# An adding transfer in place of a subtraction: remainders of every second half block of up weights

## The chip, the cores and the metric

The kernel runs on one core of a Trainium2 chip. The metric is the time of one execution in device microseconds (us); the figure for a kernel is the median of several runs. The core has five engines with instruction queues of their own, each working through its queue in order: TensorE (PE; its weight loads are listed as PEld), VectorE (DVE), ScalarE (ACT), GpSimd (POOL) and SyncE (SP). Transfers are issued from the queues of SP, ACT or POOL and carried by 16 DMA engines, which all queues share.

## The reference

Two layers of an encoder over 256 tokens of width 2048. Each layer computes a joint input projection, two groups of attention heads, an output projection, and then a gated feed-forward with a short convolution over the tokens:

```python
h2 = rms_norm(x, ln2_g[l])
u = depthwise_conv(h2 @ w_up[l], conv_w[l], conv_b[l])
gate, up = u[..., :D_FF], u[..., D_FF:]
x = x + (jax.nn.silu(gate) * up) @ w_down[l]
```

`w_up` has 2048 rows and 2 x 5632 columns in each layer. All data are float32. The change concerns only how the blocks of `w_up` are prepared for TensorE.

## The kernel before

All products run on TensorE in the type float32r, which keeps fewer bits than float32. To hold the precision, each operand is taken apart into a rounded part and a remainder: hi = round(w), lo = w - hi. A product is then the sum of hi·hi, hi·lo and lo·hi; each half block of weights is therefore needed as two tiles, `whi` and `wlo`.

The weights come in blocks of 128 x 2048 elements (1 MB), the *quanta*. The list `quanta` (lines 700 to 730) fixes their order for the whole kernel: for each layer 36 blocks of the input projection, 16 of the output projection, then in five chunks the blocks of up (two for each of 44 column blocks f), and between them those of down in three kinds (`plain`, `seven`, and the ordinary ones). Each quantum is worked off in two *steps* of half a block, 1024 columns, a `seven` in three. A step of up weights is eight pairs of matmuls (`two`, lines 411 to 414): one of 512 columns with a piece of `whi` and one of 256 columns with a piece of `wlo`.

What precedes a step's matmuls:

- `load` (line 736) loads a quantum into one of three `raw` buffers by a transfer of SP's queue. The next load is issued when the last step of the quantum has been split (`left`, lines 768 to 771), three quanta ahead.
- `split_w` (line 753) takes a half block apart: it fetches a `whi` and a `wlo` buffer, of which there are five each (`SPLIT_AHEAD + 1`), and calls `split` (line 109). There ACT rounds the half block into `whi` (line 112) and DVE subtracts this from the raw block into `wlo` (line 113).
- The main loop (lines 854 to 860) calls `split_w` four steps ahead of the matmuls. The buffers that step s + 4 gets are those that step s - 1 has read, so the rounding waits for TensorE to finish step s - 1.

After the last step of a column block f, `glu` (line 540) takes the result out of the accumulator (ACT, L546; DVE, L547 and L548), copies the edges of the convolution on POOL (L550, L551), convolves (ACT, L556; DVE, L558), applies the gate (L560, L562) and splits the result for the down products. Apart from these copies POOL computes some powers (L107) and sums of squares (L124) in the attention stage; it issues no transfer.

The order on each engine is worked out by the planner of the tile framework, from the program's order, its estimate of durations and the priorities set with `tc.high_priority`. `split_w` sets such a priority around the splitting (line 760). The framework also derives the waits from what each instruction reads and writes.

Of the kernel before, what the change touches and what calls it, by code (L numbers as in the profile page):

```python
# [12 lines left out]
F32R = mybir.dt.float32r  # L13
I32 = mybir.dt.int32
AF = mybir.ActivationFunctionType
ALU = mybir.AluOpType
# [43 lines left out]
def encoder_kernel(  # L60
# [5 lines left out]
    nc = tc.nc  # L66
# [42 lines left out]
    def split(hi, lo, src, scale=None):  # L109

        if scale is None:
            high = nc.scalar.activation(hi, src, AF.Copy)  # L112
            nc.vector.tensor_sub(lo, src, hi.bitcast(F32))  # L113
        else:
            high = nc.scalar.activation(hi, src, AF.Copy, scale=scale)  # L115
            nc.vector.scalar_tensor_tensor(lo, src, scale, hi.bitcast(F32),
                                           op0=ALU.mult, op1=ALU.subtract)
        return high
# [286 lines left out]
    quanta = []  # L405
# [122 lines left out]
    def q_up(l, f, u):  # L528
        def body(q, half, hi, lo):
            if u == 0 and half == 0:  # L530
                cur["up"] = psum.tile([P, 2, 2, T], F32, name="mm", bufs=2)
            ps = cur["up"]
            hv, lv = (w.rearrange("p (k j n) -> p k j n", k=4, j=2) for w in (hi, lo))
            for j in range(2):
                for kk in range(4):
                    k = 8 * u + 4 * half + kk
                    two(ps[:, j], hv[:, kk, j], lv[:, kk, j], xs[k], k == 0, k == KD - 1)
            if u == 1 and half == 1:
                glu(l, f, ps)
        return body  # L540
# [159 lines left out]
    for l in range(L):  # L700
# [8 lines left out]
        for c, nf in enumerate(CHUNKS):  # L709
            up = lambda f: [(a["w_up"][l, f, u], q_up(l, f, u), "up") for u in range(2)]  # L710
# [23 lines left out]
    raw, hl, left, loads, highs = {}, {}, {}, {}, {}  # L734

    def load(q, parts=1):
        if q < len(quanta):
            raw[q] = wp.tile([P, 2048], F32, name="raw", bufs=3)
            left[q] = 3 if quanta[q][2] == "seven" else 2
            m = 2048 // parts  # L740
            for j in range(parts):
                loads[q] = nc.sync.dma_start(out=raw[q][:, j * m:(j + 1) * m], in_=quanta[q][0][:, j * m:(j + 1) * m])

    def split_seven(w, part, hi, lo):

        hv, lv = (t.rearrange("p (k n) -> p k n", k=2) for t in (hi, lo))
        if part == 1:
            nc.vector.tensor_sub(w[:, 1:3], w[:, 1:3], w[:, 2:4])
            nc.vector.tensor_add(w[:, 3], w[:, 3], w[:, 1])
            nc.vector.tensor_sub(w[:, 0], w[:, 3], w[:, 0])  # L750
        return split(hv, lv, (w[:, 1::2], w[:, 1:3], w[:, 0::3])[part])

    def split_w(s, parts=1):
        if s < len(steps):
            q, half = steps[s]
            kind = quanta[q][2]
            o = UP_AT if kind == "up" else 0
            hl[s] = tuple(wp.tile([P, 1024 + 64], F32R, name=t, bufs=SPLIT_AHEAD + 1)[:, o:o + 1024]
                          for t in ("whi", "wlo"))
            with tc.high_priority(offset=AHEAD_PRIO if s >= KD // 2 else 0):  # L760
                if kind == "seven":
                    highs[s] = split_seven(raw[q].rearrange("p (k n) -> p k n", k=4), half, *hl[s])
                else:
                    m = 1024 // parts
                    for j in range(parts):
                        highs[s] = split(*(t[:, j * m:(j + 1) * m] for t in hl[s]),
                                         raw[q][:, half * 1024 + j * m:half * 1024 + (j + 1) * m])
            left[q] -= 1
            if left[q] == 0:
                del raw[q]  # L770
                load(q + LOAD_AHEAD)
# [65 lines left out]
    for i in range(SPLIT_AHEAD):  # L837
        first_x(i)
        split_w(i, 2 if i == 0 else 1)
# [14 lines left out]
    for s, (q, half) in enumerate(steps):  # L854
        if s + SPLIT_AHEAD < KD // 2:
            first_x(s + SPLIT_AHEAD)
        split_w(s + SPLIT_AHEAD)
        quanta[q][1](q, half, *hl.pop(s))
        for f, args in side.pop((q, half), []):
            f(*args)  # L860
# [101 lines left out]
```

## Time and profile before

| | |
|---|---|
| runs | 2090.13, 2090.67, 2090.73 us; median 2090.67 |
| span of the profiled execution | 2088.2 us, first to last instruction; the profile has no other time of that execution |
| DMA engines | 408.41 MB moved, mean 196 GB/s over the span |
| loads of up weights | 176 of 1024 KB, all on SP's queue |
| steps of up weights | 352, 8 x 352 = 2816 matmuls of each of the two sizes |

The profile is one execution. Busy time is the union of an engine's instructions; for TensorE the ends of pipelined matmuls are modelled, so the waits and the pace say more there than the share. "L113" is line 113 of the kernel. In the groups, `wlo<-raw,whi` means that `wlo` is written from `raw` and `whi`, `x795` is the count (a few records are missing), then busy us and mean ns, then the idle time of the engine before these instructions with what ended it.

### The profile page before, as it was taken

The page shows a single profiled execution, that of the slowest core. Times are in us where ns is not written, and L with a number is a line of the kernel's source. Part 1 is how long each engine was busy: PE and PEld are TensorE (multiplying, and loading weights), DVE is VectorE, ACT ScalarE, POOL GpSimd, SP SyncE. Part 2 cuts the span into 40 slices and gives each one's busy share as a digit, 9 for nine tenths or more (in the row PEclk, how much of TensorE's full clock was granted, in tenths as well). Part 3 has the DMA queues.
Part 4 walks back from the last instruction along what each step waited for, and adds up shares of the span by engine and source line. Part 5 has one row for each costly group of instructions (what it writes and reads, how often), then busy time and mean ns, then how long its engine had stood idle before and what let it go on. Part 6 is the DMA issues. An engine that isn't in the chain of part 4 may idle for free.

```text
span 2088.2 us, 29195 instructions
## 1 busy us (share of the span) xinstructions
PE 2082.8 (100%) x10816; PEld 1788.6 (86%) x10816; DVE 1719.4 (82%) x2604; ACT 1222.1 (59%) x1817; POOL 175.4 (8%) x237
## 2 busy tenths in 40 slices
PE   9999999999999999999999999999999999999999
PEld 8888888888888888888888888888888888888887
DVE  7786657898898988989757766578989989899896
ACT  7566556555555556556555665565656565555553
POOL 0011100100101001011000111001001010010100
PEclk9999999999999999999999999999999999999999
DMA  9544555556565564656655445555565655656554
GB/s 353 196 144 168 176 179 173 194 200 207 179 242 184 209 211 165 240 194 210 208 182 182 162 166 171 169 180 195 208 202 175 235 195 204 204 187 232 184 200 161
DMA packets 62143, 408.41 MB, mean 196 GB/s; under 512 B 7344, under 2 KB 9904, under 8 KB 13744
## 3 DMA queue, kind: packets, MB, share of 16 engines
q1 hardware_dynamic: 61280, 405.46, 56.4%
q8 instruction: 85, 1.39, 0.3%
q10 hardware_dynamic: 720, 1.08, 0.2%
q14 instruction: 58, 0.48, 0.1%
HBM read 404.42 MB, written 2.10 MB: 195 GB/s over the span
## 4 chain that ended last, share of the span: by engine, by line
PE 100%; ACT 0%; DVE 0%; issue 0%
PE mm L98 90%; PE S L98 4%; PE pv L98 3%; PE tr L98 2%; PE tr L373 1%; PE tr L307 1%; PE S L149 1%; ACT v_a L263 0%; ACT mid L115 0%; DVE x L689 0%; DVE ones L90 0%; DVE halfpi L94 0%; DVE power L92 0%
## 5 line engine op out<-in xcount | busy, mean ns | idle before, releaser
L112 ACT ACTIVATE whi<-raw 128x1024 fp32r<-128x1024 f32 (+1 forms) x797 | 830.8, 1057 | 684.3 <-PE mm L98 403.0
L113 DVE TENSOR_TENSOR wlo<-raw,whi 128x1024 fp32r<-128x1024 f32 (+1 forms) x797 | 964.8, 1221 | 271.9 <-ACT whi L112 234.6
L98 PE MATMUL mm<-xs,whi 128*128 128x512 f32 x2816 | 977.0, 390 | 0.0
L98 PE MATMUL mm<-xs,wlo 128*128 128x256 f32 x2816 | 794.1, 282 | 0.0
L98 PEld LDWEIGHTS mm<-xs,whi 128*128 128x128 f32 x2816 | 528.3, 188 | 110.5
L98 PEld LDWEIGHTS mm<-xs,wlo 128*128 128x128 f32 x2816 | 532.2, 189 | 1.1
L98 PE MATMUL mm<-whi,mid 128*128 128x512 f32 x1412 | 369.4, 391 | 0.4 <-ACT v_a L263 0.4
L98 PEld LDWEIGHTS mm<-whi,mid 128*128 128x128 f32 x1412 | 262.6, 188 | 54.5 <-ACT v_a L263 0.9
L98 PE MATMUL mm<-whi,xs 128*128 128x512 f32 x1152 | 294.7, 393 | 0.1
L98 PEld LDWEIGHTS mm<-whi,xs 128*128 128x128 f32 x1152 | 212.7, 188 | 42.6 <-ACT whi L112 0.8
L98 PE MATMUL mm<-wlo,mid 128*128 128x512 f32 x706 | 201.8, 391 | 0.0
L98 PE MATMUL mm<-wlo,xs 128*128 128x512 f32 x576 | 158.8, 392 | 0.0
L98 PEld LDWEIGHTS mm<-wlo,mid 128*128 128x128 f32 x706 | 132.2, 188 | 27.2
L558 DVE SCALAR_TENSOR_TENSOR pT<-halo,conv,pT 128x256 f32<-128x256 f32 x352 | 148.3, 480 | 0.9
L550 POOL COPY halo<-halo 128x6 f32<-128x6 f32 x88 | 40.6, 461 | 1233.6 <-DVE halo L548 1233.6
L98 PEld LDWEIGHTS mm<-wlo,xs 128*128 128x128 f32 x576 | 107.0, 188 | 21.4
L556 ACT ACTIVATE pT<-halo,conv 128x256 f32<-128x256 f32 x176 | 95.1, 588 | 5.8 <-DVE halo L548 5.7
L551 POOL COPY halo<-halo 128x6 f32<-128x6 f32 x88 | 76.0, 864 | 0.2 <-POOL halo L550 0.2
L548 DVE TENSOR_TENSOR halo<-prob,acc_b 128x512 f32<-128x512 f32 x88 | 60.7, 690 | 1.9
L547 DVE TENSOR_TENSOR prob<-prob,mm 128x512 f32<-128x512 f32 x88 | 60.0, 681 | 0.0
L546 ACT ACTIVATE prob<-mm 128x512 f32<-128x512 f32 x88 | 51.4, 584 | 7.1 <-PE mm L98 7.1
L560 ACT ACTIVATE prob<-pT 128x256 f32<-128x256 f32 x88 | 35.6, 404 | 30.3 <-DVE pT L558 30.3
(180 smaller groups left out, 1479.8 us busy)
## 6 DMA issues: line engine op xcount, KB each, us to landing
raw<-in_w_up SPq DMA_DIRECT2D x176, 1024.0 KB, 4.9
raw<-in_w_in SPq DMA_DIRECT2D x71, 1024.0 KB, 4.9
raw<-in_w_down SPq DMA_DIRECT2D x48, 1024.0 KB, 4.9
raw<-in_w_seven SPq DMA_DIRECT2D x40, 1024.0 KB, 4.9
raw<-in_w_out SPq DMA_DIRECT2D x32, 1024.0 KB, 4.8
raw<-in_w_plain SPq DMA_DIRECT2D x10, 1024.0 KB, 4.8
bias<-in_bias SPq DMA_DIRECT2D x16, 160.0 KB, 3.1
x<-in_x SPq DMA_DIRECT2D x4, 512.0 KB, 10.0
```

Of the source, the lines that this page charges most:

```text
L98: nc.tensor.matmul(ps, lhsT, rhs, start=start, stop=stop, skip_group_check=True)
L112: high = nc.scalar.activation(hi, src, AF.Copy)
L113: nc.vector.tensor_sub(lo, src, hi.bitcast(F32))
L149: nc.tensor.transpose(ps[:, j, tt * P:(tt + 1) * P], x[:, tt, (k + j) * P:(k + j + 1) * P], ident)
L546: nc.scalar.activation(t, ps[:, :, 0], AF.Copy)
L547: nc.vector.tensor_add(t, t, ps[:, :, 1])
L548: nc.vector.tensor_mul(ux[:, :, r:r + T], t, st["r2"][:, None, :].to_broadcast([P, 2, T]))
L550: nc.gpsimd.tensor_copy(ux[:, :, 1:r], ux[:, :, T:T + r - 1])
L551: nc.gpsimd.tensor_copy(ux[:, :, T + r:T + 2 * r - 1], ux[:, :, r + 1:2 * r])
L556: nc.scalar.activation(y[:, j, :], ux[:, j, r:r + T], AF.Identity, scale=w1, bias=b)
L558: nc.vector.scalar_tensor_tensor(y[:, j, :], ux[:, j, o:o + T], w, y[:, j, :], op0=ALU.mult, op1=ALU.add)
L560: nc.scalar.activation(t[:, 0, :], y[:, 0, :], AF.Silu)
```

## The change

In `split_w`, the second half (`half == 1`) of every quantum of kind "up" takes a path of its own; all other half blocks keep `split`.

```diff
             with tc.high_priority(offset=AHEAD_PRIO if s >= KD // 2 else 0):
                 if kind == "seven":
                     highs[s] = split_seven(raw[q].rearrange("p (k n) -> p k n", k=4), half, *hl[s])
+                elif kind == "up" and half == 1:
+                    hi, lo = hl[s]
+                    src = raw[q][:, 1024:2048]
+                    highs[s] = nc.scalar.activation(hi, src, AF.Copy)
+                    nc.scalar.activation(lo, src, AF.Copy, scale=-1.0)
+                    nc.gpsimd.dma_start(out=lo, in_=quanta[q][0][:, 1024:2048].bitcast(F32R), accum_op=ALU.add)
                 else:
                     m = 1024 // parts
```

ACT rounds the half block into `whi` as before, and then once more with the sign turned into `wlo`, which then holds -hi. In place of DVE's subtraction, a transfer issued on POOL's queue reads the same half block from device memory (128 rows of 4 KB, 512 KB) and adds it to `wlo`: w + (-hi). There are 2 layers x 44 column blocks x 2 quanta = 176 such half blocks. The transfer waits for the second rounding, and the matmuls that read `wlo` wait for the transfer. The raw buffer is now read by the two roundings alone.

## The prediction

> **What bounds the kernel now.** I read the page's totals and the chain that ended last, then who waited for whom on TensorE, then the stage of the up weights instruction by instruction. The totals and the chain:
>
> ```profile
> span 2088.2 us, 29195 instructions
> PE 2082.8 (100%) x10816; PEld 1788.6 (86%) x10816; DVE 1719.4 (82%) x2604; ACT 1222.1 (59%) x1817; POOL 175.4 (8%) x237
> PEclk9999999999999999999999999999999999999999
> PE 100%; ACT 0%; DVE 0%; issue 0%
> ```
>
> TensorE (PE) is the whole chain. It is not busy for 2088.2 - 2082.8 = 5.4 us, at the granted clock's top tenth throughout. Since the ends of matmuls are modelled, a full PE could hide slow matmuls, so I look for waits of PE and for its pace. The waits on PE and PEld:
>
> ```profile
> PE pv L98 <- DVE halfpi L94: 1.1, 1, 1.1
> PE mm L98 <- ACT v_a L263: 0.4, 2, 0.2
> PEld mm L98 <- ACT whi L112: 0.8, 2, 0.5
> ```
>
> Columns: total us, times, longest. Out of 352 up steps no matmul waited for wlo, and the whole list stays under 4 us. The pace stands in ScalarE's (ACT's) timeline of one up stage, since each rounding there starts when TensorE gives a buffer back:
>
> ```profile
> 503.85 1.06 ACT L112 ACTIVATE whi<-raw 128x1024 fp32r<-128x1024 f32 x1 [1.40 <-issue]
> 504.81 0.58 ACT L546 ACTIVATE prob<-mm 128x512 f32<-128x512 f32 x1
> 506.63 1.06 ACT L112 ACTIVATE whi<-raw 128x1024 fp32r<-128x1024 f32 x1 [1.24 <-PE mm L98]
> 507.60 1.08 ACT L556 ACTIVATE pT<-halo,conv 128x256 f32<-128x256 f32 x2
> 509.39 1.06 ACT L112 ACTIVATE whi<-raw 128x1024 fp32r<-128x1024 f32 x1 [0.72 <-ACT pT L556]
> ...
> 512.18 1.06 ACT L112 ACTIVATE whi<-raw 128x1024 fp32r<-128x1024 f32 x1 [1.42 <-PE mm L98]
> ...
> 514.94 1.06 ACT L112 ACTIVATE whi<-raw 128x1024 fp32r<-128x1024 f32 x1 [0.78 <-ACT mid L112]
> ```
>
> Roundings start at 503.85 and 514.94, four steps apart: 11.09 us, so a step is 2.77 us and a 1 MB up block (two steps) 5.55 us. The 176 up blocks take 176 x 5.55 = 976 us of the span. ACT and VectorE (DVE) prepare each half block four steps ahead (SPLIT_AHEAD, five buffers), so **11.09 us from the freed buffer to the matmul that reads it** is the budget of a half block. Before, it uses 1.06 us for the rounding and 1.22 us for the subtraction.
>
> **What goes away.** The group table, one row a shape:
>
> ```profile
> L113 DVE TENSOR_TENSOR wlo<-raw,whi 128x1024 fp32r<-128x1024 f32 x795 | 963.5, 1223 | 271.8 <-ACT whi L112 234.6 <-PE mm L98 29.3 <-ACT mid L115 3.8
> L112 ACT ACTIVATE whi<-raw 128x1024 fp32r<-128x1024 f32 x795 | 829.7, 1058 | 684.3 <-PE mm L98 403.0 <-DVE raw L748 88.8 <-issue 87.0
> ```
>
> 2 layers x 44 column blocks x 2 blocks x one second half = 176 subtractions of 1.223 us leave DVE: -215 us, 1719 to about 1504 (72%). DVE is not on the chain and TensorE did not wait for it, so this is worth nothing directly; what would be late next is TensorE itself. The most that any shortening can bring is that 5.4 us gap. I count **0**.
>
> **What ACT gets.** 176 more 128x1024 roundings, priced by the row above: 176 x 1.058 = +186 us, 1222 to 1408 (67%). In the stage of up weights ACT has room:
>
> ```profile
> 726.00:820.00 94.00, 94.00 (x537) 83.01 (x536) 82.31 (x126) 54.25 (x79) 8.38 (x14) 1.00 0.60 205
> ```
>
> (Columns: stretch, its us, then busy us of PE, PEld, DVE, ACT, POOL; granted clock; share of the 16 DMA engines; GB/s.) ACT is 54.25 of 94 us, 58%; one more rounding per 5.55 us adds 19 points, 77%. The budget covers it: **0**, but ACT works in order, so the second rounding can stand behind the two L556 of 1.08 us together that follow the one at 506.63. If that cover is gone the half block is ready 1.08 us later; that is a term below. The raw buffer is now given back by this rounding, 2.12 us after the start, where the subtraction gave it back at 1.06 + 1.22 = 2.28: SP's next load is released 0.2 us earlier, worth nothing by itself. But **the same event now releases both the load of 1 MB and the adding transfer**, so they run against each other.
>
> **What POOL and its queue get.** 176 DMA issues, each behind a wait for ACT. The trace of before has no transfer of POOL and none that adds. Queued behind the waiting issue on POOL are the halo copies; DVE's L558 waits for those, and behind L558 on DVE stand the first halves' subtractions. These have 11.09 us and need 2.28, so a POOL held up for a few us costs nothing. The nearest rows for the issue and its surroundings:
>
> ```profile
> L742 SPq DMA_DIRECT2D raw<-in_w_up x176: 327/328/328, 303.8 to 2011.9; - x176
> 507.62 0.19 POOL L550 COPY halo<-halo 128x6 f32<-128x6 f32 x1 [9.03 <-DVE halo L548]
> 507.74 1.26 POOL L551 COPY halo<-halo 128x6 f32<-128x6 f32 x1
> 507.73 1.23 DVE L113 TENSOR_TENSOR wlo<-raw,whi 128x1024 fp32r<-128x1024 f32 x1 [0.24 <-ACT whi L112]
> ```
>
> An issue takes SP 0.33 us. The second copy equals the first in size and takes 1.26 us, exactly while a subtraction of 1.23 us runs on DVE: POOL can be held for one DVE instruction. So an issue is 0.33 to 0.33 + 1.26 = 1.59 us; I take both ends along. The Trainium skill, "SBUF — State Buffer", "Who interferes with whom", says more narrowly that two-input subtractions hold POOL's reads only, and that the writing of descriptors for POOL's transfers is held by DVE's two-port modes (it calls this inferred). By that rule the issue would lie at the low end and the sum below at its low end, by the copy's row at its high end; no row of this trace shows an issue on POOL.
>
> **The transfer.** Its nearest rows, and the transfer engines in this stage and when full:
>
> ```profile
> raw<-in_w_up SPq DMA_DIRECT2D x176, 1024.0 KB, 4.9
> bias<-in_bias SPq DMA_DIRECT2D x16, 160.0 KB, 3.1
> x<-in_x SPq DMA_DIRECT2D x4, 512.0 KB, 10.0
> 499.00:510.00 11.00, 11.00 (x66) 9.74 (x65) 9.29 (x15) 6.35 (x10) 1.38 (x2) 1.00 0.60 194
> 30.00:41.00 11.00, 11.00 (x50) 9.11 (x49) 10.62 (x27) 9.13 (x17) 0.73 (x1) 1.00 1.02 392
> ```
>
> Full engines move 392 GB/s (the share of 1.02 early in the run, where loads queue up). So of a load's 4.9 us, 1.049 MB / 392 GB/s = 2.7 us is moving and 2.2 us is the rest. An adding transfer reads 512 KB from memory, reads 512 KB of the remainder in SBUF, and writes 512 KB. It could count as a copy of 512 KB (the two reads overlapping), as 1 MB (two reads in a row), as 1.5 MB (each pass on its own), or more if the addition itself is slow, for which no row gives an end. I take 1 MB: two reads through the unit that a copy's one read uses.
>
> The Trainium skill, "Collectives: The Full Stack", "The bandwidth ceiling: the fold count and why AG ≠ RS ≠ AR", says that an add in the DMA engines costs no cycles itself but needs two source reads, which halve the rate. It speaks against the low end; by it the landing is the one I sum, by the low end it would be 1.3 us sooner. No row here shows an addition.
>
> **The sum for one half block**, from the freed buffer, with the load running fully against it: rounding and negated rounding 2 x 1.06 = 2.12; issue 0.33 to 1.59; latency 2.2; load 2.7; adding transfer 2.7. Together **10.1 to 11.3 us against a budget of 11.09**. The first matmul that reads wlo is the second of its step; the pair of 512 and 256 columns takes 2.77 / 8 = 0.35 us, two thirds of it the first, so another 0.23 us: 11.32. Just hidden. With a plain-copy price it is 8.8 to 10.0; with 1.5 MB 11.4 to 12.6.
>
> Throughput, per up block of 5.55 us: 1.049 MB of load and 1.049 MB counted for the add, over 392 GB/s, 5.35 us, 96%. In the stage before, 194 GB/s took a share of 0.60. It fits, by 4%.
>
> **Forecast.** Both conditions are met, narrowly, and where they are met TensorE sees nothing: the span stays 2088.2 us. The median of the runs, 2090.67, is 2.5 us above this span; that stays outside the span and unchanged. **2090.7 us**, own range 2087 to 2095.
>
> **Rivals.** A measurement of this kernel tells about 0.2% (4.2 us) from no change.
>
> *Late landing (slower).* The transfer engines keep up, but a half block takes longer than 11.32 us. Then TensorE stalls once per four steps, since the buffer chain is a loop of four steps: loss = (time - 11.32) x 352 / 4 = 88 us for each us. It decides at 11.32. For it: the top of my sum touches it, and the 1.08 us of L556 would put it at 11.2 to 12.4. The 512 KB loads of x, early in the run among full engines, took 10.0 us: 2.12 + 10.0 + 0.33 = 12.45. Against it: loads and adds need not collide fully, since the load has a start on the issue of POOL. Price at 12.45: 1.13 x 88 = +99 us, **2190 us**.
>
> *The transfer engines become the bound (slower).* It decides at 5.55 x 392 = 2.18 MB per block, that is, when adding 512 KB costs more than 1.13 MB, 2.15 times its bytes. At three times: (1.049 + 1.573) / 392 = 6.69 us per block, 1.14 x 176 = +201 us, **2291 us**. At four times: 8.02 us, +2.47 x 176 = +435, 2526 us. For it: 4% of room is less than the uncertainty of every term. Against it: only 1.5 MB per block leave device memory, 1.573 / 5.55 = 283 GB/s, and 392 has been seen.
>
> *Faster.* If DVE's 215 us mattered somewhere, PE would show waits for it; they come to some 2 us in all. At most 5.4 us: **2085 us**.
>
> *No relief in substance.* Should the planner set the second rounding or the transfer late in its queue, DVE still loses its 215 us and the late landing's price applies; I count it there.
>
> **How the numbers follow.** Hidden 0.42, late landing 0.28, engines as the bound 0.28, faster 0.02. Hidden is the likeliest single case and gives the predicted time, although the two slower ones together weigh more: same 0.42, slower 0.56, faster 0.02. The range runs from 2087 to 2300: it takes in the late landing and the engines as the bound up to three times the bytes; above lie additions slower than that, about 0.15, below the 0.02.
>
> **What would show it.** Hidden: wlo's transfers on POOL's queue land within about 9 us of their issue, PE has no wait on wlo, roundings still start 11.09 us apart over four steps, the share of the DMA engines in the up stage rises from 0.60 to about 0.9, DVE falls to some 1504 us, ACT rises to 1408. Late landing: PEld waits for the transfer once per two or four steps, with the share of the engines below 1. Engines as the bound: share at 1, landings growing, loads of raw late too and ACT waiting for them. If landing is 5 us or less, the add counts as a copy and my 1 MB was too much; if POOL's issues take longer than 1.59 us, my issue term was too small.

## The result and the profile after

The changed kernel takes 2249.33 us (median of 2251.55, 2243.32 and 2249.33) against 2090.67 us: ratio 1.0754, 95% interval 1.0733 to 1.0776, so 7.5% slower. The profiled execution has a span of 2249.8 us, 161.6 us more than the span before.

The page of the changed kernel: busy time, two of the DMA queues, the chain by engine.

```profile
span 2249.8 us, 29685 instructions
PE 2137.4 (95%) x10816; PEld 1810.0 (80%) x10816; DVE 1525.9 (68%) x2428; ACT 1387.0 (62%) x1993; POOL 269.4 (12%) x413
...
q1 hardware_dynamic: 61280, 405.46, 53.0%
q0 software_dynamic: 25344, 92.29, 21.2%
...
PE 52%; DMA 26%; issue 17%; DVE 3%; ACT 2%; POOL 0%; SPq 0%; POOLq 0%; DVEq 0%; ACTq 0%
```

DVE lost 193 us and ACT gained 165, where 215 and 186 were counted by durations; busy time counts the overlapping ends of neighbours once (below, 526.54 + 1.06 is 0.10 us past the next start), so it moves a little less. Neither is on the chain. TensorE is no longer the whole chain: a quarter of it is the new transfer. ("issue" is time for which the profile shows no wait.) POOL's queue, q0, moved 92.29 MB.

TensorE's waits, and the issues of the two kinds of transfers in the up stage (last column: median us from issue to landing):

```profile
PE mm L98 <- DMA wlo<-in_w_up: 93.4, 59, 3.7
PE mm L98 <- DVE wlo L113: 5.7, 8, 1.3
...
raw<-in_w_up SPq DMA_DIRECT2D x176, 1024.0 KB, 8.6
wlo<-in_w_up POOLq DMA_DIRECT2D x176, 512.0 KB, 10.0
```

Before, no matmul waited for wlo. Now 59 do, for 93.4 us in all. An add lands 10.0 us after its issue; the loads, 4.9 us before, take 8.6.

One such wait, followed through: ACT's timeline, POOL's, and TensorE's.

```profile
526.54 1.06 ACT L766 ACTIVATE whi<-raw 128x1024 fp32r<-128x1024 f32 x1 [0.94 <-PE mm L98]
527.50 1.04 ACT L767 ACTIVATE wlo<-raw 128x1024 fp32r<-128x1024 f32 x1
```

```profile
528.95 0.88 POOL L768 DMA_DIRECT2D wlo<-in_w_up  x1 [0.90 <-ACT wlo L767]
```

```profile
537.49 0.39 PE L98 MATMUL mm<-xs,whi 128*128 128x512 f32 x1
540.90 0.58 PE L98 MATMUL mm<-xs,wlo 128*128 128x256 f32 x1 [3.02 <-DMA wlo<-in_w_up]
541.27 0.63 PE L98 MATMUL mm<-xs,whi 128*128 128x512 f32 x1
541.71 0.41 PE L98 MATMUL mm<-xs,wlo 128*128 128x256 f32 x1
541.92 0.63 PE L98 MATMUL mm<-xs,whi 128*128 128x512 f32 x1
```

The buffer was free at 526.54; the matmul that reads it could start at 540.90, 14.36 us later. The budget was 11.32 us, and 14.36 - 11.32 = 3.04 is the wait of 3.02 us. The two roundings and the 0.4 us before the issue take the first 2.41 us of it; issue and transfer take the other 11.95.

The rows after the wait show a second loss. A pair of matmuls takes 541.92 - 541.27 = 0.65 us here, where a step of 2.77 us gave 0.35. The windows around it (columns as in the prediction):

```profile
536.00:540.00 4.00, 1.88 (x11) 1.41 (x9) 2.51 (x3) 2.81 (x4) 0.31 (x2) 1.00 0.99 264
540.00:544.00 4.00, 3.10 (x10) 2.72 (x11) 1.70 (x4) 0.62 (x2) 0.86 (x1) 0.57 1.07 272
544.00:548.00 4.00, 4.00 (x25) 3.52 (x24) 1.83 (x3) 1.53 (x3) 0.00 (x0) 1.00 0.91 232
```

The granted clock is 0.57 in the 4 us after the wait and 1.00 again in the next. Over the run it is 0.984, where it was 1.000.

So the 161.6 us divide into time in which TensorE is not busy, (2249.8 - 2137.4) - 5.4 = 107.0 us, and 2137.4 - 2082.8 = 54.6 us in which the same matmuls take longer. Of the latter the clock accounts for (1 - 0.984) x 2249.8 = 36 us at most, since some of the slow time falls into waits. The other 19 us or more are not traced to a cause; the ends of matmuls are modelled, and part of them may lie there.

### The profile page after: what moved, and what is told of

It reads as the page before. It is cut to its first block, busy times and chain, and to the rows that moved or that the text cites. A ratio compares the mean times of both kernels' runs of the same rounds, so it can differ in the third digit from the quotient of the medians.

```text
span 2249.8 us, 29685 instructions
## 1 busy us (share of the span) xinstructions
PE 2137.4 (95%) x10816; PEld 1810.0 (80%) x10816; DVE 1525.9 (68%) x2428; ACT 1387.0 (62%) x1993; POOL 269.4 (12%) x413
## 3 DMA queue, kind: packets, MB, share of 16 engines
q0 software_dynamic: 25344, 92.29, 21.2%
q10 hardware_dynamic: 720, 1.08, 0.1%
## 4 chain that ended last, share of the span: by engine, by line
PE 52%; DMA 26%; issue 17%; DVE 3%; ACT 2%; POOL 0%; SPq 0%; POOLq 0%; DVEq 0%; ACTq 0%
PE mm L98 47%; DMA wlo<-in_w_up 26%; PE S L98 1%; PE pv L98 1%; DVE wlo L113 1%; ACT whi L112 1%; PE tr L373 1%; DVE halo L548 0%; DVE prob L547 0%; PE tr L98 0%; PE tr L307 0%; ACT mid L112 0%; PE S L149 0%; ACT wlo L767 0%; DMA raw<-in_w_in 0%
## 5 line engine op out<-in xcount | busy, mean ns | idle before, releaser
L113 DVE TENSOR_TENSOR wlo<-raw,whi 128x1024 fp32r<-128x1024 f32 (+1 forms) x621 | 751.5, 1221 | 416.8 <-ACT whi L112 373.3
L98 PE MATMUL mm<-xs,whi 128*128 128x512 f32 x2816 | 1008.0, 399 | 2.8 <-DVE prob L547 2.8
L112 ACT ACTIVATE whi<-raw 128x1024 fp32r<-128x1024 f32 (+1 forms) x621 | 646.1, 1055 | 514.3 <-PE mm L98 242.0
L98 PE MATMUL mm<-xs,wlo 128*128 128x256 f32 x2816 | 814.2, 290 | 99.5 <-DMA wlo<-in_w_up 93.4
L98 PEld LDWEIGHTS mm<-xs,wlo 128*128 128x128 f32 x2816 | 546.5, 194 | 126.5 <-DMA wlo<-in_w_up 115.3
L766 ACT ACTIVATE whi<-raw 128x1024 fp32r<-128x1024 f32 x176 | 186.1, 1057 | 173.3 <-PE mm L98 172.9
L768 POOL DMA_DIRECT2D wlo<-in_w_up x176 | 153.5, 872 | 1011.5 <-ACT wlo L767 618.3
L767 ACT ACTIVATE wlo<-raw 128x1024 fp32r<-128x1024 f32 x176 | 183.6, 1043 | 0.0
L98 PEld LDWEIGHTS mm<-wlo,xs 128*128 128x128 f32 x576 | 107.0, 188 | 21.4
L556 ACT ACTIVATE pT<-halo,conv 128x256 f32<-128x256 f32 x176 | 95.0, 587 | 1.3 <-DVE halo L548 1.3
L113 DVE TENSOR_TENSOR mid<-bias,mid 128x256 fp32r<-128x256 f32 x82 | 34.7, 423 | 76.3 <-ACT mid L112 76.3
L550 POOL COPY halo<-halo 128x6 f32<-128x6 f32 x88 | 36.9, 419 | 364.9 <-DVE halo L548 364.9
```

Source lines behind the costliest of these rows:

```text
L98: nc.tensor.matmul(ps, lhsT, rhs, start=start, stop=stop, skip_group_check=True)
L550: nc.gpsimd.tensor_copy(ux[:, :, 1:r], ux[:, :, T:T + r - 1])
L556: nc.scalar.activation(y[:, j, :], ux[:, j, r:r + T], AF.Identity, scale=w1, bias=b)
L766: highs[s] = nc.scalar.activation(hi, src, AF.Copy)
L767: nc.scalar.activation(lo, src, AF.Copy, scale=-1.0)
L768: nc.gpsimd.dma_start(out=lo, in_=quanta[q][0][:, 1024:2048].bitcast(F32R), accum_op=ALU.add)
```

## The experiments

Two theories stood at first. **L**: each add lands too late for a chain of four steps, whatever else runs. **S**: the 16 DMA engines have more to move than they can. After the first eight runs a third took the place of both, **C**: the engines can move it all, but an add that starts together with a load lands too late for the lead it has.

All ratios are against the kernel before on the same chip, 2090.1 to 2090.2 us.

### Every second add only (e1_fourth)

```diff
-                elif kind == "up" and half == 1:
+                elif kind == "up" and half == 1 and nth(s) % 2:
```

Here `nth` counts the calls.

> Only every second of the 176 adding transfers is left (88, one per column block); the other second halves are subtracted on DVE as before. Theory S (the 16 DMA engines are full): an up block costs them 3.05 us for its load and 2.71 us for an add, so a column block of 11.1 us now needs 2 x 3.05 + 2.71 = 8.8 us; landings fall under 9 us and the time returns to 2091 to 2100 us. Theory L (each transfer, on its own, lands later than the buffer chain of four steps allows): one late transfer in each four steps is enough to stretch them, so the time stays near that of the change, 2220 to 2250 us.

Measured: 2107.53 us, ratio 1.0087 (1.0069 to 1.0104). The waits on adds, and their landing:

```profile
PE mm L98 <- DMA wlo<-in_w_up: 9.7, 10, 2.3
...
wlo<-in_w_up POOLq DMA_DIRECT2D x88, 512.0 KB, 7.9
```

L in its first form falls: one add in every four steps doesn't stretch them. With 7.9 us an add just fits: 2.1 + 0.4 + 7.9 = 10.4 us against 11.32. Most of the loss went, but 17 us stayed, more than S expected.

### The negated rounding first (e2_negfirst)

```diff
-                    highs[s] = nc.scalar.activation(hi, src, AF.Copy)
                     nc.scalar.activation(lo, src, AF.Copy, scale=-1.0)
+                    highs[s] = nc.scalar.activation(hi, src, AF.Copy)
```

> The two roundings of ACT change places, so each transfer can start 1.06 us earlier; bytes and counts stay. Theory L: 1.0 us less on a chain that closes once in four steps, 88 of them, -90 us, about 2160 us. Theory S: the engines have as much to move as before, 2240 to 2255 us.

Measured: 2246.14 us, ratio 1.0741 (1.0699 to 1.0782), the change's own. It looks like a verdict for S, and is none. ACT's timeline:

```profile
503.68 1.06 ACT L767 ACTIVATE whi<-raw 128x1024 fp32r<-128x1024 f32 x1 [1.71 <-PE mm L98]
504.64 1.04 ACT L766 ACTIVATE wlo<-raw 128x1024 fp32r<-128x1024 f32 x1
```

Line 767 still runs ahead of line 766: the planner put the plain rounding first again, so the edit never reached the chip. The run says nothing of either theory.

### A copy in place of the add (e3_copy)

```diff
-                    nc.gpsimd.dma_start(out=lo, in_=quanta[q][0][:, 1024:2048].bitcast(F32R), accum_op=ALU.add)
+                    nc.gpsimd.dma_start(out=lo, in_=quanta[q][0][:, 1024:2048].bitcast(F32R))
```

> The transfer copies instead of adding (the remainder is left out: wlo then holds w itself); count, bytes from memory, queue and waits stay. If the addition's second read is what costs, the engine time of a transfer falls from 2.71 us to about 1.4 us, an up block needs 4.5 of 5.55 us, landings fall to 6 to 8 us, and the time is 2091 to 2110 us. If the cost lies with POOL's queue and its smaller packets and not with adding, 2.2 us and more remain and the time stays above 2200 us.

Measured: 2113.41 us, ratio 1.011 (1.0094 to 1.0125). Queue and landing, on the page:

```profile
q0 software_dynamic: 25344, 92.29, 11.9%
...
wlo<-in_w_up POOLq DMA_DIRECT2D x176, 512.0 KB, 6.0
```

The same packets and bytes take 0.119 x 2108.7 / 176 = 1.43 us of all engines per transfer; in the change it was 0.212 x 2249.8 / 176 = 2.71 us. Adding costs 1.9 times copying, which is what the prediction counted as 1 MB. The Trainium skill, "Collectives: The Full Stack", "The bandwidth ceiling: the fold count and why AG ≠ RS ≠ AR", says two source reads halve the rate; this run agrees for adds into SBUF. What remains of the loss, 23 us, is not waits on wlo's transfers: TensorE waited 0.3 us for them. 5.6 us went into eight waits for DVE's subtractions at the starts of up stages, which the change has too (5.7 us, eight times).

### The second rounding alone (e4_act)

```diff
                     nc.scalar.activation(lo, src, AF.Copy, scale=-1.0)
-                    nc.gpsimd.dma_start(out=lo, in_=quanta[q][0][:, 1024:2048].bitcast(F32R), accum_op=ALU.add)
+                    nc.vector.tensor_sub(lo, src, hi.bitcast(F32))
```

> ACT makes its second rounding into wlo as in the change, but DVE then writes the remainder over it and there is no transfer. If ACT's added 186 us lie beside TensorE's work, 2091 +- 4 us. If ACT's order pushes the following roundings late, 2100 us or more.

Measured: 2090.34 us, ratio 1.000 (0.9991 to 1.001). ACT's share of the change is free, as costed.

### Half the columns by the add (e5_half)

```diff
-                    nc.scalar.activation(lo, src, AF.Copy, scale=-1.0)
-                    nc.gpsimd.dma_start(out=lo, in_=quanta[q][0][:, 1024:2048].bitcast(F32R), accum_op=ALU.add)
+                    nc.vector.tensor_sub(lo[:, 0:512], src[:, 0:512], hi[:, 0:512].bitcast(F32))
+                    nc.scalar.activation(lo[:, 512:1024], src[:, 512:1024], AF.Copy, scale=-1.0)
+                    nc.gpsimd.dma_start(out=lo[:, 512:1024], in_=quanta[q][0][:, 1536:2048].bitcast(F32R), accum_op=ALU.add)
```

> All 176 transfers stay, each adding only 512 of the 1024 columns (256 KB); DVE subtracts the other 512. Theory S (16 DMA engines full): 3.05 + 1.36 = 4.4 us of 5.55 us per up block, so 2091 to 2115 us, as in the run with half as many transfers. If the number of transfers costs (issue, waits, order on POOL) and not their bytes, the time stays above 2170 us.

Measured: 2114.28 us, ratio 1.0115 (1.01 to 1.013). The 176 issues and waits stay, and the loss is 24 us: it is mainly the bytes that cost, not the number of transfers. (The second rounding is shorter too, 0.62 us against 1.04, so each add starts some 0.4 us sooner.) So far S had most for it, and the next run spoke against it.

### Adds on the first halves (e6_first)

```diff
-                elif kind == "up" and half == 1:
+                elif kind == "up" and half == 0:
...
-                    src = raw[q][:, 1024:2048]
+                    src = raw[q][:, 0:1024]
...
-                    nc.gpsimd.dma_start(out=lo, in_=quanta[q][0][:, 1024:2048].bitcast(F32R), accum_op=ALU.add)
+                    nc.gpsimd.dma_start(out=lo, in_=quanta[q][0][:, 0:1024].bitcast(F32R), accum_op=ALU.add)
```

> The adding transfers take the first half of each up block in place of the second; bytes and count stay. The raw buffer is then given back by the other half's subtraction, one step (2.77 us) after the add was issued, so that load and add no longer start on one event. Theory S: as much to move, 2235 to 2255 us. If it is their starting together that makes landings long, landings fall below 9 us and the time below 2180 us.

Measured: 2184.55 us, ratio 1.0448 (1.043 to 1.0465). Just above the bound written down, and 65 us below the change with the same bytes. Most of the first up stage, first of the change, then of this run:

```profile
340.00:430.00 90.00, 82.32 (x454) 71.92 (x453) 48.43 (x88) 60.60 (x84) 14.37 (x28) 0.96 0.95 244
```

```profile
340.00:430.00 90.00, 89.91 (x519) 79.43 (x518) 59.16 (x106) 67.63 (x93) 21.12 (x30) 1.00 0.97 274
```

At TensorE's pace, 32 matmuls in 5.55 us, 90 us hold 519 of them. The change does 454 there and moves 244 GB/s; this run does 519 and moves 274, near the (1.049 + 0.524) MB / 5.55 us = 283 GB/s that the pace asks for (the difference over 90 us, 0.8 MB, is less than one block). The engines are nearly full, at a share of 0.97, but they can move what TensorE needs: S as a bound of throughput falls. Landings were 7.6 us. What is left here is at the edges of the up stages and in the last chunk of each layer, with one wait each of 8.9 and 8.6 us.

### The add one step earlier (e7_early), and the price of its room (e8_room)

```diff
+    def start_lo(s):
+        if s < len(steps) and steps[s][1] == 1 and quanta[steps[s][0]][2] == "up":
+            q = steps[s][0]
+            lo = early[s] = buf("wlo", UP_AT)
+            with tc.high_priority(offset=AHEAD_PRIO):
+                nc.scalar.activation(lo, raw[q][:, 1024:2048], AF.Copy, scale=-1.0)
+                nc.gpsimd.dma_start(out=lo, in_=quanta[q][0][:, 1024:2048].bitcast(F32R), accum_op=ALU.add)
...
+        start_lo(s + SPLIT_AHEAD + 1)
         split_w(s + SPLIT_AHEAD)
```

`buf` gives wlo six buffers; pT has three in place of four and prob_a two in place of three. The run e8_room is the kernel before with these two numbers alone.

> The negated rounding and the add of a second half are issued five steps ahead in place of four (six wlo buffers; room for them comes from one pT and one prob_a buffer less). The chain then closes after 13.87 us. Theory S with a floor: an up block costs the engines 5.76 us and TensorE 5.55 us, so 0.21 x 176 = +37 us and some 20 us at the stages' edges stay, 2125 to 2160 us. If the engines already give all they can at the 6.5 us per block of the change, 2230 us and more.

> The kernel before with one pT and one prob_a buffer less and nothing else: the price of the room that the run with the earlier add takes. 2091 to 2100 us.

Measured: e7_early 2155.19 us, ratio 1.0311 (1.0296 to 1.0326); e8_room 2089.67 us, ratio 0.9998 (0.9989 to 1.0007), so the room costs nothing. The same stretch, and POOL's issues at the start of the next up stage with the wait that follows:

```profile
340.00:430.00 90.00, 90.00 (x521) 79.76 (x520) 57.30 (x103) 66.89 (x94) 15.73 (x30) 1.00 0.97 273
```

```profile
468.87 0.89 POOL L764 DMA_DIRECT2D wlo<-in_w_up  x1 [33.48 <-ACT wlo L763]
470.94 0.87 POOL L764 DMA_DIRECT2D wlo<-in_w_up  x1 [1.18 <-ACT wlo L763]
473.78 0.86 POOL L764 DMA_DIRECT2D wlo<-in_w_up  x1 [1.97 <-ACT wlo L763]
```

```profile
478.36 0.38 PE L98 MATMUL mm<-xs,wlo 128*128 128x256 f32 x1 [3.25 <-DMA wlo<-in_w_up]
```

More lead removes the waits inside the stage. At its start three adds are issued within 5 us, beside loads, and the first matmul that needs one waits 3.25 us. All ten waits on adds of over 1 us in this run come 9.5 to 10.4 us after the first add of an up stage. The number came out as expected for S with a floor of 37 us, but not for that reason: there is no floor inside the stage, since TensorE is busy for all of the 90 us there, and the rest lies at the edges.

### The order fixed (e9_forced)

```diff
-                    highs[s] = nc.scalar.activation(hi, src, AF.Copy)
-                    nc.scalar.activation(lo, src, AF.Copy, scale=-1.0)
+                    neg = nc.scalar.activation(lo, src, AF.Copy, scale=-1.0)
+                    with tc.issue_after(neg.ins):
+                        highs[s] = nc.scalar.activation(hi, src, AF.Copy)
```

> The negated rounding comes before the plain one, now with their order on ACT fixed (in the run before, the planner had put them back), so that each add starts about 1 us earlier; bytes, count and the common start with the load stay. Theory C (chain: the add lands later than the four steps of lead allow, because a load runs against it): about 1 us less on chains that close 88 times, -50 to -90 us, 2160 to 2200 us. Theory S (the engines' throughput is the bound): no change, 2240 to 2255 us.

Measured: 2197.05 us, ratio 1.0515 (1.0498 to 1.0533), -52 us. Now the order holds on the chip, and the issue follows the freed buffer by 528.30 - 526.84 = 1.46 us, where it was 2.41:

```profile
526.84 1.06 ACT L766 ACTIVATE wlo<-raw 128x1024 fp32r<-128x1024 f32 x1 [1.19 <-PE mm L98]
527.80 1.04 ACT L768 ACTIVATE whi<-raw 128x1024 fp32r<-128x1024 f32 x1
...
528.30 0.86 POOL L769 DMA_DIRECT2D wlo<-in_w_up  x1 [4.67 <-ACT wlo L766]
```

Landings stay at 9.9 us after the issue; only the start has moved by about 1 us. A bound of throughput would not have seen this.

### The load held back by a step (e10_apart)

```diff
+    held = []
+    mark = const.tile([P, 1], F32, name="mark")
...
+            while held and held[0][0] < s:
+                t, old = held.pop(0)
+                with tc.issue_after(highs[s].ins):
+                    nc.scalar.activation(mark, raw[old][:, 0:1], AF.Copy)
+                del raw[old]
+                load(old + LOAD_AHEAD)
             left[q] -= 1
             if left[q] == 0:
-                del raw[q]
-                load(q + LOAD_AHEAD)
+                if kind == "up":
+                    held.append((s, q))
+                else:
+                    del raw[q]
+                    load(q + LOAD_AHEAD)
```

> The change as it is, but the next load of a raw buffer freed by an up block waits until the following step's rounding on ACT (one 128x1 copy marks it), so that load and add no longer start on one event; bytes, count, order and lead of the add stay. Theory C with the common start as its cause: landings of wlo fall from 10.0 to about 8 us and the time to 2150 to 2190 us, as with the adds on the first halves. Theory S, or a gain there that came from something else: 2235 to 2260 us.

Measured: 2170.86 us, ratio 1.0384 (1.0355 to 1.0412), -78 us. An add, the small copy that releases the next load, and the landings:

```profile
502.63 0.86 POOL L771 DMA_DIRECT2D wlo<-in_w_up  x1 [4.70 <-ACT wlo L770]
...
504.19 0.18 ACT L780 ACTIVATE mark<-raw 128x1 f32<-128x1 f32 x1
```

```profile
raw<-in_w_up SPq DMA_DIRECT2D x176, 1024.0 KB, 7.7
wlo<-in_w_up POOLq DMA_DIRECT2D x176, 512.0 KB, 7.9
```

The load now starts some 1.7 us after the add's issue; in the change one event, the end of the second rounding, releases both. Holding a load back makes the kernel faster: adds land after 7.9 us in place of 10.0. The common start is a cause of the late landings, by a run that changes little else.

### Both mends (e11_both), and with every second add (e12_bothfourth)

The edits of e9_forced and e10_apart together, and then with that of e1_fourth as well.

> Both mends together: the negated rounding first and the load held back by one step; all 176 adds. If the two act on the same chain and add up, -52 and -78 us from 2249, 2110 to 2130 us. If what the held load leaves are the stages' edges, which neither mends, 2140 to 2170 us.

> Both mends and only every second add (88). Theory C: with landings near 8 us and 9.9 us of lead after the negated rounding no add is late inside a stage; only edges remain, 2091 to 2100 us. It cannot come under the kernel before, since TensorE has nothing to gain there: not under 2087 us.

Measured: e11_both 2146.56 us, ratio 1.0259 (1.0225 to 1.0293); e12_bothfourth 2098.79 us, ratio 1.0052 (1.0031 to 1.0074). The first page's waits, then the landing in the second:

```profile
PE mm L98 <- DMA wlo<-in_w_up: 34.7, 20, 4.3
```

```profile
wlo<-in_w_up POOLq DMA_DIRECT2D x88, 512.0 KB, 5.6
```

The two mends don't add up to -130 us; -103 us came, and the 20 waits left are mostly within the first blocks of up stages and in the last chunk, as the second expectation had it. With half the adds and no common start an add lands after 5.6 us; even then 8.7 us are lost. No version with an add came under the kernel before, as follows from TensorE having nothing to gain there.

## Why the prediction was right or wrong

The forecast, hidden at 2090.7 us with a range of its own of 2087 to 2095, did not come: the kernel took 159 us more. The rival "late landing" did, which had a chance of 0.28. The range to 2300 held the time only because it was drawn round the two slow rivals, and the direction was given as slower (0.56) while the single forecast was no change.

**What goes away: right.** DVE shed its work and TensorE gained nothing from it. No run came out faster than before by more than the measurement tells.

**What ACT gets: right.** e4_act, 2090.34 us. In the change 160 of the 176 second roundings run directly behind the first; the 1.08 us of L556, which the prediction feared between them, come after (526.54 and 527.50 above).

**The issue on POOL: in the range, but not for its reasons.** 0.87 us in the median lies within 0.33 to 1.59, and no issue took over 1.06 us:

```profile
L768 POOL DMA_DIRECT2D wlo<-in_w_up x176: 862/865/1061, 321.8 to 2185.1; - x176
```

The shortest takes 0.862 us, far from SP's 0.33; the issue of e3_copy's plain copy takes POOL 0.53. So 0.87 is the length of the adding form itself. The halo copy's 1.26 us beside a subtraction is not found in an issue: 91 of the 176 ran beside a subtraction and took 0.862 to 1.061 us, the others 0.862 to 0.920. The Trainium skill, "SBUF — State Buffer", "Who interferes with whom", says that two-input subtractions hold POOL's reads, and infers that they do not hold the writing of descriptors. These issues agree with it.

**The add counted as 1 MB: right.** 2.71 us of full engines, against the 2.7 of the sum (e3_copy gives the copy's 1.43).

**Throughput at 96%: right, by as little as it said.** In e6_first and e7_early the engines, at a share of 0.97, carry 274 and 273 GB/s with TensorE at its pace. The rival "transfer engines become the bound" did not decide. Its sign was ACT waiting for late loads; the changed kernel itself shows next to none:

```profile
ACT whi L112 <- DMA raw<-in_w_up: 4.1, 8, 1.0
```

**The sum for one half block: wrong, and this is the step that failed.** It gave the transfer 2.2 + 2.7 + 2.7 = 7.6 us when a load runs against it, behind an issue of 0.33 to 1.59: 7.9 to 9.2 us. The profile counts a landing from the start of the issue; with the 0.4 us before it that made 10.0 + 0.4 = 10.4. Four runs show what the time goes with, by their median landings:

| | load and add apart | load and add on one event |
|---|---|---|
| an add in every second block | 5.6 (e12_bothfourth) | 7.9 (e1_fourth) |
| an add in every block | 7.9 (e10_apart) | 10.0 (the change) |

The order of the roundings, mended in e12_bothfourth too, does not enter: 9.9 us in e9_forced and 8.0 in e11_both. The common start costs 2.1 to 2.3 us, which the sum had with its 2.7 for the load. Adds in every block cost as much again, 2.1 to 2.3, and for this the sum had no term: it let one add meet one load. In the changed kernel 156 of the 175 later adds were issued before the add ahead of them had landed, in e1_fourth 4 of 87. The loads grow as well, from 4.9 to 8.6 us. Whether the add ahead or the slower loads hold an add up is not taken apart here.

**The price of a late landing: right in the total of the waits, too small for the whole.** The rule, 88 us for each us over 11.32, with 2.1 for the roundings, 0.4 from there to the issue (as at 528.95 above) and 10.0 gives 12.5, so 1.18 x 88 = 104 us; TensorE's idle time grew by 107. The agreement is one of the totals: the rule has 88 equal waits, and there were 59 on adds, of 1.6 us in the mean and up to 3.7. The rival's 2190 us came near for a like reason, since it borrowed 10.0 us from the loads of x, early in the run. The 54.6 us by which the matmuls became slower were not in the sum; a wait was priced at its own length only.

**The lead.** The budget of 11.09 us was read in the middle of an up stage and used for all of it. At the stage's start several adds and loads are let go together. That is where e7_early and e11_both still wait.

## What to carry to other kernels

A transfer put on a chain of buffers needs its landing time at the load that the engines then have; near full engines the sum of its own and one neighbour's time is too short, and a term for the queue behind it belongs to it. Look at what else the same event releases: here the freed buffer started the load that the add then ran against, and holding that load back by a step was worth 78 us. After an edit of the order, read the order off the timeline before judging the result: one run here measured an edit that the planner had undone.

## What had not been expected of the hardware

TensorE's granted clock falls after waits that are short. In the changed kernel all ten waits of TensorE of over 2.75 us were followed by 2.9 to 6.1 us at about half pace (the row of 540.90 above). Of the twenty between 1.5 and 2.75 us seven were, the shortest of 1.81 us, some with a delay of up to 1.5 us; of the thirteen between 1.0 and 1.5 us none. So the length of a wait alone does not decide, and in e7_early one of 3.25 us (at 478.36) had no slow stretch behind it while nine others, of 2.87 to 3.67 us, had. No run here tests the clock by itself. Its part, at most 36 us, is a third of what the waits themselves cost.
